# Query projections as seven block products, late groups behind the residual, and two MLPs in program order

## The chip, the cores and the metric

The kernel runs on one core of a Trainium2 chip. The metric is the device time of one execution in microseconds (us). The same kernel was timed three times; the median is the figure that counts.

## The reference

The program is a two-layer decoder trunk over 1024 tokens of width 1024, in float32. Each layer is a mixer, a cross-attention into 256 memory tokens and a squared-ReLU MLP, each behind an RMS norm and with a residual add. Layer 0 mixes by differential attention and pooling, layer 1 by a gated short convolution.

```python
def cross_attention(h, mem_n, wq, wkv, wo):
    q = (h @ wq).reshape(B, S, X_HEADS, X_HEAD_DIM)          # 1024 x 1024 @ 1024 x 1024, 4 heads of 256
    kv = (mem_n @ wkv).reshape(B, M, 2, X_HEADS, X_HEAD_DIM)
    s = jnp.einsum('bshd,bmhd->bhsm', q, kv[:, :, 0]) * X_HEAD_DIM ** -0.5
    p = jax.nn.softmax(s, axis=-1)
    o = jnp.einsum('bhsm,bmhd->bshd', p, kv[:, :, 1]).reshape(B, S, D_MODEL)
    return o @ wo

def sq_relu_mlp(h, w1, w2):                                  # 1024 -> 4096 -> 1024
    a = jax.nn.relu(h @ w1)
    return (a * a) @ w2

# layer l:  h += mixer(rms_norm(h)); h += cross_attention(rms_norm(h), ...); h += sq_relu_mlp(rms_norm(h), ...)
```

## The kernel before

**Operands.** The hidden state is kept transposed: 8 tiles of 128 features by 1024 tokens. Every operand of a large product is cut into a high part (rounded, by ACT) and a low part (the rest, by DVE, `cut`), and a product takes three matmuls: high by high, high by low, low by high. Weights are loaded in an order written out once (`order`); `w_load` keeps up to four raw tiles in flight on the SP queue, and `w_cut` cuts one weight tile ahead of its use into two rotating buffers (`wh`, `wl`). `w_next` hands out the next cut tile and cuts one more.

**Plain products.** `gemm` computes one 128-feature output tile: 8 input tiles x 3 parts x 2 halves of 512 tokens, so 48 matmuls of 128x512 (L189). The query projections of both cross-attentions, the output projections and the convolution's projections are of this kind.

**Block products.** Both MLP products go by `split_gemm` (L265): two output tiles and two token halves make a 2x2 block, got from seven products of sums of blocks instead of eight. One call has 7 steps of 4 x 3 = 12 matmuls. The sums of weight blocks are formed on POOL inside `w_cut` (L149 to L153, four operations of 128x512 for a pair of weight tiles), the sums of activation blocks on DVE in `combine`; `Split` holds the four groups of cut activations. After step i, `out(i)` adds the step's PSUM bank into its result (`evac`), as listed in `ADDS`; the banks are few, so step i+2 often has to wait until step i's bank was read. Hooks, small functions keyed by step, are run ahead of a step's matmuls and place other work there: the norm's transposes (`stage1`, `stage2`), squares and stores of the MLP's first product, loads and cuts of its second product's operand.

**The residual** (`residual`) runs an output projection, adds the loaded hidden state, and prepares the next operand: with `split=True` the four groups of a `Split`, pair by pair of tiles, otherwise plain cut tiles. The two residuals ahead of the MLPs are split; the two ahead of the cross-attentions (named `X1` and `cvo`) are not. In the last tile of a split residual the halves are done one after the other, then all four groups, the last squares of the norm and the store follow.

**Cross-attention** (`cross`): `query(n)` for n = 0 to 6, `score(0)`, `query(7)`, and then eight units (4 heads x 2 token halves) of score, softmax, transpose and product with V. `kv_get(c)` loads the keys and values of two heads and cuts them, the low part on POOL (L873): once after query 3, once after `score(1)`.

**Order.** The order of instructions on each engine comes from a scheduler that plays the program through with modelled durations and picks by priority (the program's order) what is ready. Only the first stage is under `tc.manual_schedule(engines=IN_ORDER)`, where PE, DVE and ACT take the program's order. All activations live in 44 slots of 128x1024.

## Time and profile before

| | us |
|---|---|
| median of three runs | 2615.15 (2613.42 to 2619.64) |
| profiled execution | 2622.43 |
| its span, first to last instruction | 2620.6 |
| PE busy | 2541.0 (97%) |
| DVE / ACT / POOL busy | 1641.9 (63%) / 1009.8 (39%) / 694.4 (26%) |

The profile is one execution. PE is the matmul engine, DVE the vector, ACT the scalar, POOL the GpSimd engine, SP issues DMAs. A row of the timeline has its start, its duration, the engine, the line of the kernel and `output<-inputs`; a bracket at its end tells how long the engine was idle before it, and who ended that. The clock column of a stage is the share of the full matmul clock that was granted. Names carry the stage: `c0q` are the queries of cross-attention 0, `c0s` its scores, `c0po` its product with V, `c0o` its residual, `m0a` and `m0b` the first and second product of MLP 0; `c1` and `m1` are those of layer 1.

### The profile page before, as it was taken

The page shows a single profiled execution, that of the slowest core. Times are in us where ns is not written, and L with a number is a line of the kernel's source. Part 1 is how long each engine was busy: PE and PEld are TensorE (multiplying, and loading weights), DVE is VectorE, ACT ScalarE, POOL GpSimd, SP SyncE. Part 2 cuts the span into 40 slices and gives each one's busy share as a digit, 9 for nine tenths or more (in the row PEclk, how much of TensorE's full clock was granted, in tenths as well). Part 3 has the DMA queues.
Part 4 walks back from the last instruction along what each step waited for, and adds up shares of the span by engine and source line. Part 5 has one row for each costly group of instructions (what it writes and reads, how often), then busy time and mean ns, then how long its engine had stood idle before and what let it go on. Part 6 is the DMA issues. An engine that isn't in the chain of part 4 may idle for free.

```text
span 2620.6 us, 29978 instructions
## 1 busy us (share of the span) xinstructions
PE 2541.0 (97%) x11618; PEld 2076.6 (79%) x11618; DVE 1641.9 (63%) x1846; ACT 1009.8 (39%) x1389; POOL 694.4 (26%) x417
## 2 busy tenths in 40 slices
PE   7999999999999999999999999999999999999997
PEld 5777778888878888777788888888887888777786
DVE  7777764325567778877773333323566777877875
ACT  4554564225443334433342111222443433433432
POOL 3222100200233334323352111111032333422334
PEclk9999999999999999999999999999999999999998
DMA  5101146311324445777742111422133344777752
GB/s 170 33 25 49 52 160 211 112 66 51 114 89 144 149 161 212 282 266 248 256 143 73 49 49 51 145 82 70 49 121 113 141 158 159 261 268 241 264 203 95
DMA packets 108430, 365.89 MB, mean 140 GB/s; under 512 B 12416, under 2 KB 14848, under 8 KB 108288
## 3 DMA queue, kind: packets, MB, share of 16 engines
q1 hardware_dynamic: 74880, 252.82, 28.7%
q10 hardware_dynamic: 33408, 111.16, 11.1%
q8 instruction: 91, 1.49, 0.2%
q14 instruction: 51, 0.42, 0.1%
HBM read 249.91 MB, written 114.03 MB: 139 GB/s over the span
## 4 chain that ended last, share of the span: by engine, by line
PE 81%; DVE 7%; issue 6%; DMA 3%; ACT 2%; SPq 0%; POOL 0%; DVEq 0%; ACTq 0%; POOLq 0%
PE m1a_x L265 7%; PE m0a_x L265 7%; PE m1a_yz L265 5%; PE m0a_yz L265 5%; PE m1b_x L265 5%; PE m0b_x L265 4%; PE m1b_yz L265 4%; PE cvo L189 3%; PE X L189 3%; PE c0o L189 3%; PE c1o L189 3%; PE m0b_yz L265 3%; PE c1q L189 3%; PE c0q L189 3%; PE qkv L189 3%
## 5 line engine op out<-in xcount | busy, mean ns | idle before, releaser
L72 ACT ACTIVATE wh<-wr 128x1024 fp32r<-128x1024 f32 (+1 forms) x310 | 301.0, 971 | 953.5 <-PE m0b_yz L265 154.9
L73 DVE TENSOR_TENSOR wl<-wr,wh 128x1024 fp32r<-128x1024 f32 (+1 forms) x310 | 361.5, 1166 | 210.6 <-ACT wh L72 209.8
L152 POOL TENSOR_TENSOR wr<-wr,wr 128x512 f32<-128x512 f32 x63 | 88.7, 1408 | 703.0 <-DVE wl L73 703.0
L73 DVE TENSOR_TENSOR wl<-wt,wh 128x1024 fp32r<-128x1024 f32 x64 | 135.7, 2120 | 4.8 <-ACT wh L72 4.6
L153 POOL TENSOR_TENSOR wr<-wr,wt 128x512 f32<-128x512 f32 x63 | 125.8, 1997 | 0.0
L150 POOL TENSOR_TENSOR wt<-wr,wt 128x512 f32<-128x512 f32 x63 | 119.9, 1904 | 4.8
L149 POOL TENSOR_TENSOR wt<-wr 128x512 f32<-128x512 f32 x63 | 90.5, 1436 | 92.0 <-issue 65.3
L72 ACT ACTIVATE wh<-wt 128x1024 fp32r<-128x1024 f32 x64 | 67.4, 1054 | 55.6 <-PE m0b_x L265 20.4
L1117 POOL TENSOR_TENSOR cv_z<-cv_z,cv_cg 128x1024 f32<-128x1024 f32 x8 | 26.2, 3276 | 175.4 <-DVE cv_z L1116 175.4
L565 ACT ACTIVATE s_p<-s,s_negm 128x128 f32<-128x128 f32 (+7 forms) x64 | 47.2, 740 | 29.1 <-DVE s_negm L564 26.1
L976 DVE SCALAR_TENSOR_TENSOR m1a_r<-m1a_r,c1o_rbc 128x1024 f32<-128x1024 f32 x32 | 52.2, 1636 | 0.9
L976 DVE SCALAR_TENSOR_TENSOR m0a_r<-m0a_r,c0o_rbc 128x1024 f32<-128x1024 f32 x32 | 52.2, 1636 | 0.9
L977 ACT ACTIVATE m1a_r<-m1a_r 128x1024 f32<-128x1024 f32 x32 | 33.9, 1061 | 42.6 <-DVE m1a_r L976 42.6
L977 ACT ACTIVATE m0a_r<-m0a_r 128x1024 f32<-128x1024 f32 x32 | 33.9, 1061 | 42.4 <-DVE m0a_r L976 42.4
L308 POOL TENSOR_TENSOR X_acc<-X_acc,X_sq 128x1024 f32<-128x1024 f32 x7 | 17.5, 2497 | 123.2 <-ACT X_sq L307 123.2
L564 DVE TENSOR_REDUCE s_negm<-s 128x1 f32<-128x128 f32 (+7 forms) x64 | 46.5, 749 | 0.2
L843 DVE TENSOR_TENSOR X1h<-X1h,X 128x1024 f32<-128x1024 f32 x8 | 9.8, 1221 | 58.0 <-PE X L189 58.0
L843 DVE TENSOR_TENSOR cvoh<-cvoh,cvo 128x1024 f32<-128x1024 f32 x8 | 9.8, 1221 | 57.3 <-PE cvo L189 57.3
L991 DVE TENSOR_TENSOR m1a_r<-m1a_r,m1a_yz 128x512 f32<-128x512 f32 x32 | 22.0, 686 | 36.6 <-PE m1a_yz L265 36.6
L991 DVE TENSOR_TENSOR m0a_r<-m0a_r,m0a_yz 128x512 f32<-128x512 f32 x32 | 22.0, 687 | 36.6 <-PE m0a_yz L265 36.6
L577 DVE SCALAR_TENSOR_TENSOR s_p<-s_p,rden,s_p 128x128 f32<-128x128 f32 (+7 forms) x32 | 36.0, 1125 | 6.4 <-ACT s_p L576 6.2
L308 POOL TENSOR_TENSOR c1o_acc<-c1o_acc,c1o_sq 128x1024 f32<-128x1024 f32 x6 | 15.5, 2588 | 91.0 <-ACT c1o_sq L307 91.0
(2717 smaller groups left out, 7986.9 us busy)
## 6 DMA issues: line engine op xcount, KB each, us to landing
wr<-in_w_dram SPq DMA_DIRECT2D x128, 512.0 KB, 3.8
m0f<-m0a_d SPq DMA_DIRECT2D x48, 512.0 KB, 5.9
m1f<-m1a_d SPq DMA_DIRECT2D x48, 512.0 KB, 6.1
wr<-in_wkv_dram SPq DMA_DIRECT2D x32, 512.0 KB, 3.5
m0a_d<-m0a_r ACTq DMA_DIRECT2D x32, 512.0 KB, 2.9
m1a_d<-m1a_r ACTq DMA_DIRECT2D x32, 512.0 KB, 2.9
wr<-in_conv_in_dram SPq DMA_DIRECT2D x24, 512.0 KB, 3.5
wr<-in_wq_dram SPq DMA_DIRECT2D x16, 512.0 KB, 3.6
```

The lines of the kernel that those rows point to most:

```text
L72: nc.scalar.activation(hi, src, AF.Copy)
L73: nc.vector.tensor_sub(lo, src, f32(hi))
L149: nc.gpsimd.tensor_add(t[:, 4:], b[:, :4], b[:, 4:])
L150: nc.gpsimd.tensor_sub(t[:, :4], a[:, :4], t[:, 4:])
L152: nc.gpsimd.tensor_sub(a[:, :4], b[:, :4], a[:, :4])
L153: nc.gpsimd.tensor_add(a[:, 4:], a[:, 4:], t[:, :4])
L189: nc.tensor.matmul(ps, wt[:, k, :], act.part(k, i, h), start=(k == 0 and wt is hi and i == 0), stop=(k == ks - 1 and wt is lo))
L265: nc.tensor.matmul(banks[b], w[a][:, 4 * (i % 2) + j, :], act.part(g, s, j, c), start=(new and j == 0 and n == 0), stop=(j == nk - 1 and n ...
L564: nc.vector.tensor_reduce(s["negm"][:, m : m + 1], ps[:, :L], axis=AX.X, op=ALU.max, negate=True)
L565: nc.scalar.activation(s["pr"][m][:, :L], ps[:, :L], AF.Exp, bias=s["negm"][:, m : m + 1], accum_out=s["den"][:, m : m + 1])
L976: nc.vector.scalar_tensor_tensor(v, v, 0.0, b(), op0=ALU.max, op1=ALU.mult)
L977: nc.scalar.activation(t, t, AF.Square)
```

## The change

1. `wq` is loaded in pairs of tiles with their features in the order that block products need, and `query(p)` makes two output tiles by one `split_gemm`: four calls of 84 matmuls in place of eight products of 48, in each of the two layers. The residuals `X1` and `cvo` are split. Their input `Y` becomes `Halves`: a slot holds the high and low part of one token half, so that slots come free half by half.
2. In the last tile of a split residual, groups 2 and 3, the norm's last squares and the store are left for hooks of steps 2, 3 and 4 of the next block product (`X.late`); one more weight cut is put there (`w_cut`). The MLP's `stage1` moves from step 4 to step 5.
3. `kv_get` runs at steps 2 and 4 of the last query pair, its low parts on DVE; `score(0)` stands ahead of that pair's last step.
4. `out` runs under `tc.high_priority()`.
5. Both MLPs are under `manual_schedule`: PE, DVE and ACT in the program's order.

```diff
-        order += [(FLAT, wq[l, n]) for n in range(KT)]
+        order += [(FLAT, wq[l, 2 * p], wq[l, 2 * p + 1]) for p in range(KT // 2)]
...
+    class Halves(Act):
+        def put(self, name, k, src):
+            t = [slot(f"{name}{k}_{h}", F32R) for h in range(2)]
+            self.t[k] = t
+            for h in range(2):
+                cut(t[h][:, :H], t[h][:, H:], src[:, half(h)])
+        def part(self, k, i, h):
+            return self.t[k][h][:, i * H : (i + 1) * H]
...
         def out(i):
-            for n, h in (TAIL_ADDS if tail else ADDS)[i]:
-                evac(n, h, banks[(TAIL if tail else SPLIT)[i][2]], (n, h) not in seen)
-                seen.add((n, h))
+            with tc.high_priority():
+                for n, h in (TAIL_ADDS if tail else ADDS)[i]:
+                    evac(n, h, banks[(TAIL if tail else SPLIT)[i][2]], (n, h) not in seen)
+                    seen.add((n, h))
...
                     if h == 0:
                         nx.group(0, j, r[0])
                         nn.add(t[:, half(h)], h, last=True)
+                    else:
+                        w_cut()
...
-                for g, raw in ((1, tt), (2, r[1]), (3, t4[:, :H])):
-                    nx.group(g, j, raw)
+                nx.group(1, j, tt)
+                if n < KT - 1:
+                    nx.group(2, j, r[1])
+                    nx.group(3, j, t4[:, :H])
             if split and n == KT - 1:
-                nn.add(t[:, half(1)], 1, last=True)
-            h_store(n, t, name)
+                nx.late = {2: [lambda: nx.group(2, j, r[1])], 3: [lambda: nn.add(t[:, half(1)], 1, last=True)],
+                           4: [lambda: nx.group(3, j, t4[:, :H]), lambda: h_store(n, t, name)]}
+            else:
+                h_store(n, t, name)
...
-                nc.gpsimd.tensor_sub(kvp[cc][1], t, f32(kvp[cc][0]))
+                nc.vector.tensor_sub(kvp[cc][1], t, f32(kvp[cc][0]))
...
-        def query(n):
-            ps = gemm(X, f"{name}q{n}", {5: nrm.stage1} if n == 0 else None)
-            Q.t[n] = pair(f"{name}q{n}")
-            cut(*Q.t[n], ps)
+        def query(p, hooks):
+            r = [slot(f"{name}q{p}_r{n}") for n in range(2)]
+            for n in range(2):
+                Q.t[2 * p + n] = pair(f"{name}q{2 * p + n}")
+            def evac(n, h, ps, new):
+                q, d = [x[:, half(h)] for x in Q.t[2 * p + n]], r[n][:, half(h)]
+                if (n, h) == (1, 0):
+                    cut(*q, ps)
+                elif new:
+                    nc.scalar.activation(d, ps, AF.Copy)
+                else:
+                    nc.vector.tensor_add(d, d, ps)
+                    if (n, h) == (1, 1):
+                        cut(*q, d)
+                    elif h == 1:
+                        cut(*Q.t[2 * p], r[0])
+            split_gemm(X, f"{name}q{p}", evac, hooks, first=(p == 0))
...
-        score(0)
-        query(KT - 1)
+        for p, hooks in enumerate((merged(X.late, {5: [nrm.stage1]}), {1: [divide]}, {},
+                                   {2: [lambda: kv_get(0)], 4: [lambda: kv_get(1)], 6: [lambda: score(0)]})):
+            query(p, hooks)
         norm_p(0)
         for u in range(n + 1):
             if u + 1 < n:
                 score(u + 1)
-                if u == 0:
-                    kv_get(1)
...
-        rest, ahead = {4: [nrm.stage1], 6: [nrm.stage2]}, []
+        rest, ahead = merged(X.late, {5: [nrm.stage1], 6: [nrm.stage2]}), []
...
-        Y = Act()
+        Y = Halves()
...
-        return residual(Y, g_next, f"{name}o")
+            Y.put(f"{nm}g", j, y)
+        return residual(Y, g_next, f"{name}o", split=True)
...
-    X, nrm = mlp(0, X, nrm, G_MIX[1], "m0")
+    with tc.manual_schedule(engines=IN_ORDER):
+        X, nrm = mlp(0, X, nrm, G_MIX[1], "m0")
```

The second MLP is put under `manual_schedule` in the same way.

More of the change, by code (lines that the diff above doesn't have):

```diff
@@ L289, in split_gemm, with merged @@
                 out(i)
+    def merged(*hooks):
+        return {i: [f for h in hooks for f in h.get(i, ())] for i in range(7)}
     class Norm:
@@ L795, in hybrid_trunk @@
             k = (0, 1, 2, 4, 5, 6, 7, 3)[i // YGAP]
-            Y.t[k] = pair(f"Y{k}")
-            cut(*Y.t[k], o_t[k] if k < 4 else y_t[k - 4])
+            Y.put("Y", k, o_t[k] if k < 4 else y_t[k - 4])
     hd = {n: xT[n] for n in range(KT)}
@@ L854, in residual @@
                 combine(r[0], r[1], tt, t4[:, :H])
-                for g, raw in ((1, tt), (2, r[1]), (3, t4[:, :H])):
-                    nx.group(g, j, raw)
+                nx.group(1, j, tt)
+                if n < KT - 1:
+                    nx.group(2, j, r[1])
+                    nx.group(3, j, t4[:, :H])
             if split and n == KT - 1:
-                nn.add(t[:, half(1)], 1, last=True)
-            h_store(n, t, name)
+                nx.late = {2: [lambda: nx.group(2, j, r[1])], 3: [lambda: nn.add(t[:, half(1)], 1, last=True)],
+                           4: [lambda: nx.group(3, j, t4[:, :H]), lambda: h_store(n, t, name)]}
+            else:
+                h_store(n, t, name)
         return nx, nn
-    X, nrm = residual(Y, G_X[0], "X1")
+    X, nrm = residual(Y, G_X[0], "X1", split=True)
     def cross(l, X, nrm, g_next, name):
@@ L872, in kv_get, with divide @@
                 nc.scalar.activation(kvp[cc][0], t, AF.Copy)
-                nc.gpsimd.tensor_sub(kvp[cc][1], t, f32(kvp[cc][0]))
+                nc.vector.tensor_sub(kvp[cc][1], t, f32(kvp[cc][0]))
         rc = small.tile([P, KT], F32, tag="rc16", name=f"{name}_rc16")
         Q = Act()
-        def query(n):
-            ps = gemm(X, f"{name}q{n}", {5: nrm.stage1} if n == 0 else None)
-            Q.t[n] = pair(f"{name}q{n}")
-            cut(*Q.t[n], ps)
-            if n == 1:
-                nc.vector.tensor_scalar_mul(rc, nrm.rcol, 1.0 / 16.0)
-            if n == 3:
-                kv_get(0)
-        for n in range(KT - 1):
-            query(n)
+        def query(p, hooks):
[15 more added lines that the diff above has]
+            split_gemm(X, f"{name}q{p}", evac, hooks, first=(p == 0))
+        def divide():
+            nc.vector.tensor_scalar_mul(rc, nrm.rcol, 1.0 / 16.0)
         units = [(h, th) for h in range(4) for th in range(2)]
@@ L1024, in ready @@
             return run
-        def merged(*hooks):
-            return {i: [f for h in hooks for f in h.get(i, ())] for i in range(7)}
         def prepare(c, left):
@@ L1105, in conv_mixer @@
         hooks = with_norm(nrm)
-        Y = Act()
+        Y = Halves()
         for j in range(KT):
@@ L1126, in conv_mixer @@
             nc.vector.tensor_mul(y, y, psb_)
-            Y.t[j] = pair(f"{nm}g")
-            cut(*Y.t[j], y)
-        return residual(Y, g_next, f"{name}o")
+            Y.put(f"{nm}g", j, y)
+        return residual(Y, g_next, f"{name}o", split=True)
     X, nrm = cross(0, X, nrm, G_MLP[0], "c0")
-    X, nrm = mlp(0, X, nrm, G_MIX[1], "m0")
+    with tc.manual_schedule(engines=IN_ORDER):
+        X, nrm = mlp(0, X, nrm, G_MIX[1], "m0")
     X, nrm = conv_mixer(X, nrm, G_X[1], "cv")
     X, nrm = cross(1, X, nrm, G_MLP[1], "c1")
-    _, fn = mlp(1, X, nrm, None, "m1")
+    with tc.manual_schedule(engines=IN_ORDER):
+        _, fn = mlp(1, X, nrm, None, "m1")
     SHARED = (4, 5)
@@ L1202, in _layout @@
     g["conv_out"] = tiles(a["conv_w_out"][0])
-    g["wq"] = tiles(a["xattn_wq"])
     g["wkv"] = a["xattn_wkv"].reshape(2, 4, 2, P, 4, H).transpose(0, 4, 1, 3, 2, 5)
@@ L1207, in _layout @@
     halves = [0, 2, 4, 6, 1, 3, 5, 7]
+    g["wq"] = tiles(a["xattn_wq"])[..., halves, :]
     g["w1"] = tiles(a["mlp_w1"])[..., halves, :]
     g["w2"] = tiles(a["mlp_w2"].reshape(2, 4, D, D))[..., halves, :]
-    return {n: np.ascontiguousarray(v) for n, v in g.items()}
+    names = ("xT memT vecs lams rel onehot negrow invcnt w_qk0 w_in w_out pool_w conv_in conv_out "
+             "wq wkv wo w1 w2").split()
+    return {n: np.ascontiguousarray(g[n]) for n in names}
 def kernel(**inputs):
```

## The prediction, made before the changed kernel was run

> **What bounds the kernel now.** I read the busy line, then the chain that ended last, then the stages, and last the timeline at each place where a stage is longer than its matmuls.
>
> ```profile
> PE 2541.0 (97%) x11618; PEld 2076.6 (79%) x11618; DVE 1641.9 (63%) x1846; ACT 1009.8 (39%) x1389; POOL 694.4 (26%) x417
> PE 81%; DVE 7%; issue 6%; DMA 3%; ACT 2%; SPq 0%; POOL 0%; DVEq 0%; ACTq 0%; POOLq 0%
> ```
>
> PE has 97% of the span and 81% of the chain: a matmul that goes away is worth its own time, unless its neighbours stop fitting under PE. The table by stage (length, then busy us per engine, the clock third from the end) tells where PE loses time today:
>
> ```profile
> core 0: us, PE busy (x) PEld busy (x) DVE busy (x) ACT busy (x) POOL busy (x), PEclk, DMA share, GB/s
> 421.14:508.18 87.04, 87.04 (x385) 72.12 (x385) 26.72 (x22) 24.17 (x25) 14.93 (x6) 1.00 0.43 150
> 508.18:585.07 76.89, 76.89 (x345) 63.76 (x344) 19.43 (x19) 16.91 (x18) 8.98 (x4) 1.00 0.21 69
> 585.07:653.41 68.34, 62.84 (x379) 55.44 (x378) 41.83 (x77) 34.16 (x89) 4.75 (x2) 0.95 0.16 55
> 746.07:772.36 26.29, 23.13 (x97) 18.73 (x96) 16.91 (x19) 9.99 (x15) 6.04 (x4) 0.87 0.18 60
> 772.36:1059.04 286.68, 286.68 (x1262) 235.45 (x1261) 222.04 (x214) 116.20 (x141) 104.64 (x60) 1.00 0.48 170
> 1059.04:1380.22 321.18, 309.60 (x1346) 251.20 (x1345) 245.02 (x249) 127.09 (x139) 116.68 (x67) 1.00 0.67 237
> ```
>
> The residual `X1` (421 to 508) and the queries (508 to 585) have no idle PE and a DVE used for a quarter to a third. Attention (585 to 653) loses 5.5 us and some clock. The seam into the MLP (746 to 772) loses 3.2 us and runs at 0.87 of the clock. The MLP's first product loses nothing, with DVE at 222 of 287 us. The second (1059 to 1380) leaves PE idle for 11.6 us. Layer 1 repeats these stages nearly to the tenth.
>
> **The change part by part.** The profiled execution took 2622.4 us (span 2620.6), 7.3 above the median of 2615.15; I sum against the former and carry the difference over.
>
> *Fewer matmuls.* One plain output tile, one step of a block product, one plain query stage; then DVE's cut of a tile and its add of a half out of PSUM, as groups:
>
> ```profile
> 1414.68 10.88 PE cv1c L189 x48
> 775.24 2.72 PE m0a_yz L265 x12
> 515.86 68.94 PE c0q L189 x304
> L73 DVE TENSOR_TENSOR wl<-wr,wh 128x1024 fp32r<-128x1024 f32 x9 | 11.0, 1225 | 59.8 <-ACT wh L72 59.8
> L991 DVE TENSOR_TENSOR m1a_r<-m1a_r,m1a_yz 128x512 f32<-128x512 f32 x32 | 22.0, 686 | 36.6 <-PE m1a_yz L265 36.6
> ```
>
> The first three give 0.2267 us a matmul. Eight query tiles are 384 matmuls, four block products are 336: 48 x 0.2267 = 10.9 us a layer, 21.8 in all. What comes with it: per pair three and a half weight cuts and two query tiles' cuts of 1.2 us and three adds of 0.7, 8.7 us of DVE, and four POOL sums, in 19 us of PE. The MLP's first product carries more per pair (222/15 = 14.8 of 19.1) with no idle PE, so I cost it at nothing; uncovered it would be 8 x 8.7 us.
>
> *Keys and values.* This is where attention loses its time, shown by DVE's, POOL's and PE's timelines and the chain:
>
> ```profile
> 588.19 1.22 DVE L908 TENSOR_REDUCE c0s_mx<-c0s 128x4 f32<-128x1024 f32 x1
> 592.23 1.14 DVE L922 TENSOR_SCALAR c0s_p<-c0s_p,c0rd 128x256 f32<-128x256 f32 x4
> 607.60 5.33 DVE L922 TENSOR_SCALAR c0s_p<-c0s_p,c0rd 128x256 f32<-128x256 f32 x4
> 607.51 2.40 POOL L873 TENSOR_TENSOR c0kv1l<-c0kv,c0kv1h 128x1024 fp32r<-128x1024 f32 x1 [44.42 <-ACT c0kv1h L872]
> 609.86 2.40 POOL L873 TENSOR_TENSOR c0kv3l<-c0kv,c0kv3h 128x1024 fp32r<-128x1024 f32 x1
> 614.99 0.80 PE L943 MATMUL c0po<-c0pt0l,c0kv2h 128*128 128x512 f32 x1 [4.58 <-DVE c0pt0l L73]
> 614.99 5.06 PE c0po L943 x11
> 631.67 2.88 PE c0s L904 x24
> ```
>
> The same four scalings take 1.14 us alone and 5.33 while POOL cuts keys: DVE is held until both POOL operations (2 x 2.40) are over, the cut of the first probabilities queues behind it, and PE waits 4.6 us. Then 11 matmuls take 5.06 us in place of 2.5, the clock being down after the wait. Together 7.1 us, and layer 1 shows the same. [...]
>
> With the low parts on DVE this goes. The four loads move up past SP's loads of the output weights, into the last query pair. `score(0)` needs the first keys at that pair's step 6, 4 x 2.72 = 10.9 us after the hook; a load takes 4.5 us to land, two cuts about 2.3:
>
> ```profile
> c0kv<-kv_d SPq DMA_DIRECT2D x4, 512.0 KB, 4.5
> ```
>
> The four DVE cuts (4.9 us) lie in the last pair, whose DVE load becomes some 15 of 19 us. What is late next is the first softmax. From its reduce to the end of the scalings it takes 593.37 - 588.19 = 5.2 us; before, query 7 (10.9 us) and the next score covered that, now only step 6 and the next score (2.72 + 2.88 = 5.6). It just fits, unless the last query's cuts stand in front of the reduce. Bounds: 0, and the 7.1 of today as the nearest wait at that place; I take 1 us, nearer to the cover that fits. So -12.2 for both layers.
>
> *Seams into the queries.* `X1` and `cvo` become split residuals, with 4 sums and 1.5 more cuts a pair in stages where DVE is used 27 of 87 us: hidden (uncovered some 4 x 4.6 us each). `Halves` turns a cut of 1.2 into two of 0.7 for eight tiles, in stages with the same idle DVE; priority and load order add no instruction and no byte. At their end the queries start as the MLP starts today. Today's plain seam costs 0, the MLP's seam this much (ACT's queue, then PE):
>
> ```profile
> 750.79 1.06 ACT L72 ACTIVATE c0o_x_3h<-c0o_r 128x1024 fp32r<-128x1024 f32 x1 [0.73 <-DVE c0o_r L249]
> 751.75 1.04 ACT L72 ACTIVATE wh<-wr 128x1024 fp32r<-128x1024 f32 x1
> 752.70 0.61 ACT L72 ACTIVATE c0o_x<-c0o_t 128x512 fp32r<-128x512 f32 x1
> 753.22 0.61 ACT L307 ACTIVATE c0o_sq<-c0oh 128x512 f32<-128x512 f32 x1
> 753.74 0.57 ACT L987 ACTIVATE m0a_r<-m0a_x 128x512 f32<-128x512 f32 x1
> 754.36 0.80 PE L265 MATMUL m0a_x<-c0o_x_0h,wh 128*128 128x512 f32 x1 [3.16 <-ACT m0a_r L987]
> ```
>
> PE waits 3.16 us for one copy out of PSUM that stands behind groups 2 and 3, a weight cut and a square, and the stage's clock of 0.87 costs 0.13 x 23.1 = 3.0 more: 6.2. These groups, the square and the store are just what is now left for later, and the copy has priority. Bounds 0 and 6.2; 1.5 each, nearer to nothing, since the copy's blockers are named and moved: +3.0.
>
> *Seams into the MLPs.* The same 6.2 goes, twice. But `stage1` now stands one step ahead of `stage2` in place of two, and PE, held to the program, must wait for the norm between them:
>
> ```profile
> 764.07 0.68 DVE L317 TENSOR_REDUCE c0o_ms<-c0o_n 128x4 f32<-128x512 f32 x1
> 765.04 1.65 POOL L320 TENSOR_TENSOR c0o_rcol<-c0o_ms,mhalf 128x8 f32<-128x8 f32 x1 [13.24 <-DVE c0o_ms L319]
> ```
>
> Two reduces and the power are 0.7 + 0.7 + 1.65 = 3.0 us against a step of 2.72, and a DVE add of 0.7 comes first: 1 us of wait (0, or 3 if two POOL sums stand ahead). Net -5.2 twice: -10.4.
>
> *First product in the program's order.* One pair of the steady state, on DVE, POOL and ACT:
>
> ```profile
> 904.21 1.23 DVE L976 SCALAR_TENSOR_TENSOR m0a_r<-m0a_r,c0o_rbc 128x1024 f32<-128x1024 f32 x1
> 907.20 1.88 DVE L976 SCALAR_TENSOR_TENSOR m0a_r<-m0a_r,c0o_rbc 128x1024 f32<-128x1024 f32 x1
> 909.01 2.32 DVE L73 TENSOR_TENSOR wl<-wt,wh 128x1024 fp32r<-128x1024 f32 x1
> 911.46 1.29 POOL L149 TENSOR_TENSOR wt<-wr 128x512 f32<-128x512 f32 x1 [1.22 <-issue]
> 912.83 2.17 POOL L150 TENSOR_TENSOR wt<-wr,wt 128x512 f32<-128x512 f32 x1
> 909.12 1.06 ACT L977 ACTIVATE m0a_r<-m0a_r 128x1024 f32<-128x1024 f32 x1 [1.64 <-DVE m0a_r L976]
> 911.53 1.06 ACT L72 ACTIVATE wh<-wr 128x1024 fp32r<-128x1024 f32 x1 [0.87 <-PE m0a_yz L265]
> ```
>
> Today the rescalings (L976) run before the third weight tile is cut; the program puts the second one behind it. From the start of step 2, in order: weight high 1.06, weight low 1.22, rescaling 1.23, ACT's square 1.06, and only then ACT's copy 0.57, which step 4 needs 2 x 2.72 = 5.44 later. The chain is 5.14: it fits by 0.3. But beside POOL a DVE operation is longer by 1.10 (2.32 for 1.22) or 0.65 (1.88 for 1.23). In program order the cut of `wt` goes on as today, from 1.1 us into the pair to 3.4; L149 comes after it, waits for a rescaling (to 4.6), and L150 ends near 7.1. The weight's low part could start at 5.44 + 1.06 + 0.1 = 6.6 and is held for 0.5: 0.2 too late. Bounds: 0, and two holds of 1.1 less 0.3, 1.9. I take 0.2, by the order just worked out: 15 pairs x 2 MLPs x 0.2 = +6.0. Behind that copy on ACT stand only the next weight's high part and the stores' DMAs, which have a step to spare.
>
> *Second product in the program's order.* PE's waits today are for the adds out of PSUM:
>
> ```profile
> PE m0b_yz L265 <- DVE m0b1h L1064: 1.9, 2, 1.4
> m0f<-m0a_d SPq DMA_DIRECT2D x48, 512.0 KB, 5.9
> ```
>
> They fall where a new quarter of the operand begins. There, in program order, DVE has in five steps (13.6 us): five cuts of 1.22, four of half that, three weight cuts and five adds, 6.1 + 2.4 + 3.7 + 3.4 = 15.6, and up to three holds of 1.1 by POOL: 18.9. Less the 13.6 and the 2 by which an add may be late (2.72 less its 0.7), that is 0 to 3.3 us. Four quarters: 0 to 13, and today's 11.6 lies inside. Loads (5.9 us) are issued three steps (8.2 us) ahead, so a cut held to its place waits for none, unless SP's queue is 2 us late. I take no change: 0, with -11.6 and, since the quarter before may leave DVE behind, +6 as ends per MLP.
>
> Sum: -21.8 - 12.2 + 3.0 - 10.4 + 6.0 + 0 = -35.4; 2622.4 - 35.4 = 2587.0 for an execution like the profiled one, 2615.2 - 35.4 = 2579.8 against the median.
>
> **The rivals.** *Order helps the second product.* Its adds no longer stand behind the scheduler's misjudged cuts: both MLPs lose 11.6 less, 2579.8 - 23.2 = 2556.6. For it: every wait there is for a DVE add, at boundaries that repeat alike. Against: DVE's load at a boundary exceeds PE's.
>
> *The seams do not close.* Scheduling outside the MLPs still follows modelled durations, which do not know POOL's hold. The queries start as the MLPs did (6.2 twice in place of 3.0: +9.4), and attention waits for its first probabilities as long as before (7.1 in place of 1, twice: +12.2): 2601.4. For it: today's scheduler made both waits; against: the blockers are moved. A PE wait of 3.16 us was enough to bring the stage's clock to 0.87. [...]
>
> *Slower: POOL holds the program's order.* If two POOL sums fall into the chain of every first-product pair, each pair loses 1.9 us: 30 x 1.9 = 57 in place of 6, 2630.8. From 1.6 us a pair on the change is slower by over 0.3%. For it: 2.32 and 1.88 show two holds in each pair today; against: the chain begins only at step 2, when L149 is mostly over.
>
> *The order does not bind*, and the MLPs run as today, seams included: 2579.8 + 10.4 - 6.0 = 2584.2; same range.
>
> **How the numbers follow.** Forecast 0.52 (2570 to 2592), order helps 0.20, seams stay open 0.12, the order does not bind 0.08, POOL holds 0.08. The range takes in the second and third with some spread and leaves out the slower rival: 2553 to 2606. A measurement of this kernel can tell 0.3%, 7.8 us: faster means under 2607.3, slower above 2623.0. Faster: all of the first, second and fourth, and half of the third, 0.86. The rest of the third and a weak form of the hold are no change, 0.08; slower 0.06.
>
> **What would show it.** Queries of 76 us a layer with PE busy throughout; no POOL row beside the scalings, each near 1.14 us, no 4.6 us wait for `c0pt0l`; the copy out of step 0 at both kinds of seam within 0.3 us of its matmuls, clock near 1.00 there; the first product's pairs at 19.2 us, with waits for ACT's copy at step 4. I am wrong if these waits exceed 1 us, if DVE waits for `m0f` loads in its order, or if the second product's idle time leaves 0 to 18 us.

## The result, and the profile after

| | median of the runs, us | ratio to before | 95% interval |
|---|---|---|---|
| before | 2615.82 (2613.42 to 2619.64) | | |
| after | 2598.22 (2597.53 to 2598.74) | 0.9931 | 0.9914 to 0.9948 |

The change gains 17.6 us, where 35.4 were forecast. The two profiled executions, 2622.4 and 2598.7 us, differ by 23.7; the kernel before spreads over 10 us from run to run (its medians in the four later comparisons are 2620.4, 2619.6, 2617.2 and 2619.8), and its granted clock goes with that: there the executions under 2618 us had a clock of 0.992 to 0.994, those above it 0.989 to 0.992. The working below goes by stages of the profiled executions, since these can be laid side by side.

The busy line of the page after, and the windows of the kernel after, each from the first matmul of a stage to the first of the next (columns as in the prediction's table: start:end, length, busy us, the clock third from the end): residual `X1`, queries, attention, first and second product of MLP 0, convolution mixer.

```profile
PE 2515.8 (97%) x11522; PEld 2055.6 (79%) x11522; DVE 1687.0 (65%) x1972; ACT 1067.7 (41%) x1503; POOL 688.7 (27%) x439
420.21:501.81 81.60, 81.60 (x362) 67.57 (x360) 46.15 (x39) 35.48 (x43) 18.18 (x8) 1.00 0.44 155
501.81:583.85 82.04, 80.50 (x358) 65.90 (x356) 50.07 (x53) 34.80 (x47) 26.98 (x16) 1.00 0.24 77
583.85:635.39 51.54, 48.65 (x313) 44.31 (x312) 35.91 (x73) 31.59 (x83) 0.00 (x0) 0.93 0.18 63
727.35:1047.19 319.84, 316.17 (x1386) 258.07 (x1384) 221.84 (x238) 130.78 (x159) 98.61 (x67) 0.99 0.46 159
1047.19:1367.75 320.56, 308.24 (x1346) 251.24 (x1344) 240.43 (x247) 123.08 (x137) 110.40 (x67) 1.00 0.64 234
1367.75:1632.77 265.02, 263.16 (x1169) 217.79 (x1168) 91.07 (x83) 47.04 (x52) 53.32 (x19) 1.00 0.19 60
```

PE lost 96 matmuls (11618 to 11522) and 25 us of busy time. The same lengths for every kernel, in us, are the thread through the rest, a block of numbers per layer. "Start" is the length of the first stage, in which the change alters hardly more than how `Y` is cut. "Queries" is residual plus queries, `cv` the convolution mixer, `m1a` and `m1b` the products of MLP 1; the tail runs from the last norm's first transposes to the end. The residuals between attention and MLP are left out: they take 91.9 to 92.2 us in every kernel. The attention column begins with the first scores, so it holds 48 matmuls of the last query in the kernel before, 36 in 2 and 9, and 12 in the others; compare queries and attention by their sum.

| kernel | start | queries | attention | m0a | m0b | cv | queries 1 | attention 1 | m1a | m1b | tail |
|---|---|---|---|---|---|---|---|---|---|---|---|
| before | 421.0 | 164.1 | 62.5 | 319.5 | 321.0 | 262.9 | 164.1 | 62.5 | 319.8 | 318.5 | 20.7 |
| after | 420.2 | 163.6 | 51.5 | 319.8 | 320.6 | 265.0 | 163.7 | 50.8 | 319.6 | 316.4 | 21.7 |
| 1 late sums | 420.6 | 162.1 | 49.4 | 315.6 | 320.5 | 265.0 | 162.0 | 51.4 | 315.6 | 316.4 | 21.3 |
| 2 early score | 419.6 | 158.3 | 55.3 | 319.8 | 320.5 | 265.0 | 158.3 | 55.5 | 318.3 | 316.5 | 21.7 |
| 3 no order | 419.9 | 163.7 | 50.5 | 315.7 | 321.0 | 262.9 | 163.7 | 51.5 | 315.8 | 317.7 | 20.7 |
| 4 keys on POOL | 419.7 | 163.7 | 48.1 | 320.7 | 320.5 | 265.0 | 163.7 | 48.1 | 319.5 | 316.4 | 21.4 |
| 5 no priority | 420.6 | 163.7 | 50.5 | 318.1 | 320.5 | 266.6 | 163.7 | 50.5 | 320.8 | 316.4 | 21.7 |
| 6 no POOL sums | 420.7 | 161.8 | 50.8 | 314.4 | 307.8 | 266.6 | 161.8 | 51.6 | 314.4 | 305.0 | 20.9 |
| 7 = 1 + 4 | 422.2 | 162.0 | 48.1 | 315.6 | 320.6 | 266.6 | 162.0 | 48.1 | 315.6 | 316.4 | 20.9 |
| 8 = 7 + 3 | 418.2 | 162.0 | 48.1 | 314.3 | 321.0 | 263.0 | 162.0 | 48.1 | 314.3 | 317.1 | 20.7 |
| 9 = 8 + 2 | 423.1 | 156.6 | 54.5 | 314.3 | 320.5 | 263.0 | 156.5 | 57.1 | 314.3 | 317.4 | 20.7 |
| 10 = 8, sums on DVE | 419.6 | 162.0 | 48.1 | 315.7 | 316.5 | 263.0 | 162.0 | 48.1 | 315.8 | 307.9 | 20.7 |
| 11 = 10 with order | 419.9 | 162.0 | 48.1 | 319.3 | 325.1 | 265.0 | 162.0 | 48.1 | 319.2 | 322.8 | 21.3 |
| 12 = 10, second product only | 418.8 | 162.0 | 48.1 | 314.6 | 317.7 | 263.0 | 162.0 | 48.1 | 314.6 | 308.1 | 20.7 |

Queries and attention together gained 11.4 us in layer 0 and 12.2 in layer 1; the two first products, which hold the MLP seams, gained nothing (+0.3 and -0.2).

**The seam into the MLP, after.** First the chain of waits' two entries, PE's and the norm's, then DVE, POOL, ACT and PE in order of time:

```profile
PE m0a_yz L277 <- DVE m0a_r L1025: 3.4, 1, 3.4
PE c0o_b L345 <- POOL c0o_rcol L336: 0.3, 1, 0.3
...
736.69 1.78 DVE L261 TENSOR_TENSOR c0o_r<-c0o_r 128x512 f32<-128x512 f32 x1
738.39 1.75 DVE L262 TENSOR_TENSOR c0o_t<-c0o_r,c0o_t 128x512 f32<-128x512 f32 x1
740.07 1.21 DVE L73 TENSOR_TENSOR c0o_x_3l<-c0o_t,c0o_x_3h 128x1024 fp32r<-128x1024 f32 x1
741.20 0.67 DVE L1025 TENSOR_TENSOR m0a_r<-m0a_r,m0a_yz 128x512 f32<-128x512 f32 x1
...
736.59 1.33 POOL L149 TENSOR_TENSOR wt<-wr 128x512 f32<-128x512 f32 x1 [5.54 <-issue]
738.00 1.60 POOL L150 TENSOR_TENSOR wt<-wr,wt 128x512 f32<-128x512 f32 x1
...
737.99 0.60 ACT L1021 ACTIVATE m0a_r<-m0a_x 128x512 f32<-128x512 f32 x1
...
741.93 0.79 PE L277 MATMUL m0a_yz<-c0o_x_0h,wh 128*128 128x512 f32 x1 [3.36 <-DVE m0a_r L1025]
742.52 0.63 PE L277 MATMUL m0a_yz<-c0o_x_0l,wh 128*128 128x512 f32 x1
```

ACT's copy, which the kernel before waited for, now runs at 737.99, while PE is still at the next bank. PE waits 3.36 us (3.16 before) for the evacuation behind it: DVE's add at 741.20. It stands behind the last two sums of `combine` and a cut of group 1, and the sums take 1.8 us each beside POOL's weight sums. The matmuls that follow come every 0.43 us in place of 0.23 until 745.07.

**Attention, after:** PE's wait, then DVE and ACT around the first softmax.

```profile
PE c0s L939 <- ACT c0s_p L948: 2.3, 2, 2.2
...
586.06 1.22 DVE L895 TENSOR_TENSOR c0kv1l<-c0kv,c0kv1h 128x1024 fp32r<-128x1024 f32 x1
587.19 1.22 DVE L943 TENSOR_REDUCE c0s_mx<-c0s 128x4 f32<-128x1024 f32 x1
588.44 0.16 DVE L944 TENSOR_TENSOR c0s_mx<-c0s_mx,c_rc 128x4 f32<-128x4 f32 x1
...
595.42 1.14 DVE L957 TENSOR_SCALAR c0s_p<-c0s_p,c0rd 128x256 f32<-128x256 f32 x4
...
589.44 1.06 ACT L72 ACTIVATE wh<-wr 128x1024 fp32r<-128x1024 f32 x1 [2.28 <-PE c0q_x L277]
...
592.36 0.55 ACT L948 ACTIVATE c0s_p<-c0s,c0s_mx,c_rc 128x256 f32<-128x256 f32 x1
```

The scalings take their 1.14 us and no 4.6 us wait is left, as forecast. But the maximum is ready at 588.6 and the first exponential starts at 592.36: ACT holds a weight cut that waits 2.28 us for PE's last query step, and behind it three cuts of the last query tiles.

**Two more waits after**, at the start of the queries and behind MLP 0:

```profile
PE c0q_yz L277 <- DVE c0q_r L912: 1.5, 1, 1.5
...
PE m0b_n L332 <- POOL m0b_acc L324: 1.9, 1, 1.9
```

### The profile page after: what moved, and what is told of

Same layout as the page of the kernel before. It is cut to its first block, busy times and chain, and to the rows that moved or that the text cites. A ratio compares the mean times of both kernels' runs of the same rounds, so it can differ in the third digit from the quotient of the medians.

```text
span 2597.0 us, 30119 instructions
## 1 busy us (share of the span) xinstructions
PE 2515.8 (97%) x11522; PEld 2055.6 (79%) x11522; DVE 1687.0 (65%) x1972; ACT 1067.7 (41%) x1503; POOL 688.7 (27%) x439
## 5 line engine op out<-in xcount | busy, mean ns | idle before, releaser
L73 DVE TENSOR_TENSOR wl<-wr,wh 128x1024 fp32r<-128x1024 f32 (+1 forms) x318 | 373.2, 1174 | 98.9 <-ACT wh L72 98.5
L152 POOL TENSOR_TENSOR wr<-wr,wr 128x512 f32<-128x512 f32 x71 | 106.0, 1493 | 792.3 <-DVE wl L73 788.3
L149 POOL TENSOR_TENSOR wt<-wr 128x512 f32<-128x512 f32 x71 | 126.3, 1779 | 135.7 <-issue 88.1
L73 DVE TENSOR_TENSOR wl<-wt,wh 128x1024 fp32r<-128x1024 f32 x72 | 146.5, 2035 | 17.0 <-ACT wh L72 17.0
L150 POOL TENSOR_TENSOR wt<-wr,wt 128x512 f32<-128x512 f32 x71 | 105.9, 1492 | 5.3
L153 POOL TENSOR_TENSOR wr<-wr,wt 128x512 f32<-128x512 f32 x71 | 105.5, 1485 | 0.0
L201 PE MATMUL X<-Y,wh 128*128 128x512 f32 x256 | 69.8, 389 | 0.0
L201 PEld LDWEIGHTS X<-Y,wh 128*128 128x128 f32 x256 | 48.0, 188 | 10.2 <-DVE X1h L851 0.3
L324 POOL TENSOR_TENSOR c0o_acc<-c0o_acc,c0o_sq 128x1024 f32<-128x1024 f32 x6 | 15.5, 2591 | 119.5 <-ACT c0o_sq L323 119.5
L201 PE MATMUL X<-Y,wl 128*128 128x512 f32 x128 | 40.7, 389 | 0.0
```

The source lines that it names most:

```text
L73: nc.vector.tensor_sub(lo, src, f32(hi))
L149: nc.gpsimd.tensor_add(t[:, 4:], b[:, :4], b[:, 4:])
L150: nc.gpsimd.tensor_sub(t[:, :4], a[:, :4], t[:, 4:])
L152: nc.gpsimd.tensor_sub(a[:, :4], b[:, :4], a[:, :4])
L153: nc.gpsimd.tensor_add(a[:, 4:], a[:, 4:], t[:, :4])
L201: nc.tensor.matmul(ps, wt[:, k, :], act.part(k, i, h), start=(k == 0 and wt is hi and i == 0), stop=(k == ks - 1 and wt is lo))
```

## The experiments

Medians are compared with the kernel after (2598.22, ratio 0.9931); each ratio is to the kernel before, timed beside it. That kernel's median was 1.4 to 4.6 us higher in these comparisons than beside the kernel after, so by the ratios each kernel comes out better by as much; differences of a few us are read by stage.

**1. Two of the four sums and group 1 later.**

```diff
-                combine(r[0], r[1], tt, t4[:, :H])
-                nx.group(1, j, tt)
+                combine1(r[0], r[1], tt)
                 if n < KT - 1:
+                    combine2(r[0], r[1], tt, t4[:, :H])
+                    nx.group(1, j, tt)
                     nx.group(2, j, r[1])
...
-                nx.late = {2: [lambda: nx.group(2, j, r[1])], 3: ...
+                nx.late = {2: [lambda: nx.group(1, j, tt), lambda: combine2(r[0], r[1], tt, t4[:, :H]),
+                               lambda: nx.group(2, j, r[1])], 3: ...
```

> Edit: at the end of a split residual only the first two of the four sums of its last pair of tiles (those of group 1) stay in front; the other two sums, and the cuts of groups 1 and 2, go behind step 2 of the next product. Theory (the wait at the seam is the queue of VectorE in front of its add, two sums of 1.8 us that POOL's sums stretch and a cut of 1.2 us): the add comes about 4.5 us earlier, PE's 3.36 us wait in front of the first steps of each MLP falls under 1 us, and the steps at the low clock after it go too: 4 to 5 us at each of the two MLP seams, up to 1 us at each query seam, 8 to 12 us in all (ratio to the changed kernel 0.9953 to 0.997; about 2586 to 2590 us). Rival A (the wait moves on: step 2 or 3 then needs group 1 or 2, cut later): PE waits as long one step further on, within 3 us of the changed kernel. Rival B (the seam is held by POOL's sums themselves, not by what stands in VectorE's queue): the wait stays on the same add and nothing moves.

2585.9 us, ratio 0.9872 (0.9858 to 0.9885): 12.3 less than after. DVE and PE at the same seam, and the first product's window:

```profile
732.79 0.68 DVE L259 TENSOR_TENSOR c0o_t<-c0o_t,c0o_r 128x512 f32<-128x512 f32 x1
735.38 0.69 DVE L1032 TENSOR_TENSOR m0a_r<-m0a_r,m0a_yz 128x512 f32<-128x512 f32 x1 [1.91 <-PE m0a_yz L282]
...
736.12 0.50 PE L282 MATMUL m0a_yz<-c0o_x_0h,wh 128*128 128x512 f32 x1 [0.85 <-DVE m0a_r L1032]
...
724.05:1039.65 315.60, 314.44 (x1385) 257.01 (x1384) 219.95 (x238) 130.70 (x159) 98.24 (x67) 1.00 0.47 161
```

DVE now waits for PE in front of the add, PE waits 0.85 us in place of 3.36, and the matmuls behind that wait come every 0.23 us (clock of the window 1.00, 0.99 in the kernel after). The first products lose 4.2 and 4.0 us, both query stages 1.6. The theory holds in place and size (8 to 12 us were expected; these stages give 11.4), and both rivals fall. The attentions moved by -2.1 and +0.6, with their clocks: 0.93 and 0.97 in the kernel after, 1.00 and 0.93 here (-2.3 and +0.9 us of PE busy time).

**2. The first scores two steps earlier.**

```diff
-  {2: [lambda: kv_get(0)], 4: [lambda: kv_get(1)], 6: [lambda: score(0)]}
+  {2: [lambda: kv_get(0)], 4: [lambda: score(0), lambda: kv_get(1)]}
```

> Edit: the first scores are computed behind step 4 of the last pair of query tiles, ahead of the load of the second keys and values, instead of behind step 6. Theory (PE's 2.3 us wait at the start of the attention, and the 0.84 us behind it, is the first softmax, whose exponentials stand in ACT's queue behind the cuts of the last query tiles): with the scores two steps earlier and the exponentials ahead of those cuts, PE still has query steps to run; about 3 us less in each layer, 5 to 6.5 us in all (about 2592 to 2593 us). Rival A (the scalings now stand in front of VectorE's last adds of the query, which come 4 to 5 us later and hold a bank or the cut that a later score needs): the wait comes back in front of the scores, no change within 2 us. Rival B (the second unit's softmax is what is late): only the 2.3 us moves on, no change.

2598.33 us, ratio 0.9916 (0.9903 to 0.993): no change that the intervals can tell; by stage, queries and attention are 1.6 and 0.7 us shorter, which is within the scatter of the attention (2.2 us, see 4). PE's wait in the attention, and DVE's first scalings and two maxima:

```profile
PE c0s L939 <- ACT c0s_p L948: 2.7, 1, 2.7
...
580.93 1.23 DVE L943 TENSOR_REDUCE c0s_mx<-c0s 128x4 f32<-128x1024 f32 x1 [0.26 <-PE c0s L939]
...
584.98 1.14 DVE L957 TENSOR_SCALAR c0s_p<-c0s_p,c0rd 128x256 f32<-128x256 f32 x4
...
593.51 1.22 DVE L943 TENSOR_REDUCE c0s_mx<-c0s 128x4 f32<-128x1024 f32 x1
```

The first softmax is over at 586, long before PE needs it. Now PE waits 2.7 us for the second unit's exponentials, whose maximum stands on DVE behind the cuts of keys, weights and query tiles. Rival B.

**3. No program order in the MLPs.**

```diff
-    with tc.manual_schedule(engines=IN_ORDER):
-        X, nrm = mlp(0, X, nrm, G_MIX[1], "m0")
+    X, nrm = mlp(0, X, nrm, G_MIX[1], "m0")
```

(and likewise for MLP 1)

> Edit: the two blocks that hold the MLPs' instructions on PE, VectorE and ACT in the program's order are taken out, all else as changed. Forecast on record: the first product pays about 6 us for the order (0.2 us a pair), the second nothing, so without the order about 6 us faster (2592 us). By the changed trace's own periods (19.16 us a pair against 19.04) it would be 3.6 us at most. Rival A (the order helps the second product's quarter boundaries, where 2 us a layer came): 3 to 10 us slower. Rival B (the planner's order is the same, but for a few instructions): within 2 us. Rival C (the seams into the MLPs need the order): the 6.2 us seams get longer, and that alone makes it slower.

2588.62 us, ratio 0.9881 (0.9867 to 0.9894): 9.6 less. Waits at the MLP seam, the mixer's window, and POOL's first norm sum there, without and then with the order:

```profile
PE m0a_yz L277 <- DVE m0a_r L1025: 1.6, 1, 1.6
...
1362.80:1625.74 262.94, 262.94 (x1170) 217.87 (x1168) 90.61 (x83) 46.45 (x52) 52.02 (x19) 1.00 0.18 59
...
1363.30 2.54 POOL L324 TENSOR_TENSOR m0b_acc<-m0b_acc,m0b_sq 128x1024 f32<-128x1024 f32 x1 [8.66 <-ACT m0b_sq L323]
```

```profile
1369.92 6.59 POOL L324 TENSOR_TENSOR m0b_acc<-m0b_acc,m0b_sq 128x1024 f32<-128x1024 f32 x2 [9.37 <-ACT m0b_sq L323]
```

The first products gain 4.1 and 3.9. Counted by the steps from matmul to matmul beyond 0.2267 us, 3.3 of the 4.1 is the seam: the scheduler lets PE go on with more of the other steps, so it waits 1.6 us there for the same add. The pairs give 0.8, not 3. The mixer gives back 2.1 and the tail 1.0. In the mixer PE's norm waits for POOL's sum, which starts 2.2 us after the mixer's first matmul with the order and 0.5 without. The second products pay 0.5 and 1.3. So the order cost the change about 9 us; the forecast's 6 was sought in the pairs, and none of the theories named more than a part of the rest.

**4. Keys' and values' low parts on POOL, at the new place.**

```diff
-                nc.vector.tensor_sub(kvp[cc][1], t, f32(kvp[cc][0]))
+                nc.gpsimd.tensor_sub(kvp[cc][1], t, f32(kvp[cc][0]))
```

> Edit: the low parts of keys and values go back to POOL, but stay where the change put them (behind steps 2 and 4 of the last query pair). Theory (the engine matters: POOL's subtraction beside the scalings stretched them, and PE waited for them): 2 to 3 us slower in each layer, 4 to 6 us in all (about 2603 us). Rival (the place was all of it: two steps earlier POOL is done before the first scalings, and VectorE has two cuts less in front of the first maximum): within 2 us, or 1 to 3 us faster.

2593.18 us, ratio 0.9897 (0.9884 to 0.9911): 5.0 less. PE's wait, DVE, POOL and ACT around the first maximum, and the attention's window:

```profile
PE c0s L939 <- ACT c0s_p L948: 1.7, 1, 1.7
...
586.52 1.23 DVE L943 TENSOR_REDUCE c0s_mx<-c0s 128x4 f32<-128x1024 f32 x1 [0.78 <-PE c0s L939]
587.78 0.96 DVE L944 TENSOR_TENSOR c0s_mx<-c0s_mx,c_rc 128x4 f32<-128x4 f32 x1
...
586.33 2.40 POOL L895 TENSOR_TENSOR c0kv3l<-c0kv,c0kv3h 128x1024 fp32r<-128x1024 f32 x1 [2.97 <-ACT c0kv3h L894]
...
589.76 0.56 ACT L948 ACTIVATE c0s_p<-c0s,c0s_mx,c_rc 128x256 f32<-128x256 f32 x1
...
583.45:631.57 48.12, 45.89 (x314) 41.52 (x312) 34.45 (x69) 29.89 (x81) 2.40 (x1) 1.00 0.18 62
```

The rival holds, with more than it asked for: the attentions are 3.4 and 2.7 us shorter. POOL is done at 588.7, before any scaling, and costs DVE 0.8 us there: the small product of 0.16 us takes 0.96 and ends with POOL. So moving the loads did all the good. How the cuts on DVE did harm is only in part shown. Two of them, of 1.2 us, stood ahead of the first two maxima, yet the first maximum was ready at 588.6, and here at 588.7. What differs is ACT: its first exponential starts at 589.76 in place of 592.36, with one cut between PE's last query step and it in place of four, since the scheduler ordered ACT anew too. Of the 3.4 us in layer 0, 2.8 are busy time of the same matmuls (48.65 to 45.89), at a clock of 0.93 after and 1.00 here. With these cuts on DVE the attention took 49.4 to 51.6 us in five kernels (the one after, 1, 3, 5 and 6), at clocks of 0.93 and 0.97 in the one after, 1.00 and 0.93 in 1, 0.97 in 5; on POOL it takes 48.1 each time (clock 1.00 in 4, 7 and 8), unless the scores come early (9).

**5. No priority for the evacuations.**

```diff
-            with tc.high_priority():
-                for n, h in (TAIL_ADDS if tail else ADDS)[i]:
+            for n, h in (TAIL_ADDS if tail else ADDS)[i]:
```

> Edit: the seven block products' evacuations without the high priority, all else as changed. Theory (the priority only matters where the planner chooses, that is at the end of a stage into the queries; inside the MLPs the program's order holds): up to 1.5 us more at each query seam and 1 us in the attention, nothing in the MLPs: 1 to 5 us slower than the changed kernel (2597 span). Rival A (the planner had put the copies in time without it, since the groups behind them are now later in the program): within 1 us. Rival B (the priority pulls adds ahead of cuts that PE needs sooner): 1 to 4 us faster.

2597.86 us, ratio 0.9918 (0.9905 to 0.9932): no change, rival A. The query stages are the same to 0.1 us. Attention, `m0a`, `m1a` and the mixer moved by up to 1.7 us either way, with the same waits in `m0a` and the mixer; these are the stages that wait 1.86 to 3.4 us in the kernel after, see the last section.

**6. POOL's weight sums left out.**

```diff
                 raw.append(t)
-                nc.gpsimd.tensor_add(t[:, 4:], b[:, :4], b[:, 4:])
-                nc.gpsimd.tensor_sub(t[:, :4], a[:, :4], t[:, 4:])
                 cut(hi, lo, a)
-                nc.gpsimd.tensor_sub(a[:, :4], b[:, :4], a[:, :4])
-                nc.gpsimd.tensor_add(a[:, 4:], a[:, 4:], t[:, :4])
```

(In place of the scratch tile `t`, the raw tile `b` is appended. The kernel leaves the sums out, so its products of the third and fourth weight groups are of other numbers; it only prices the sums.)

> Edit: POOL's four sums on each weight tile of the seven products are left out (the third and fourth weight groups then hold the raw tile, so the products of those groups are of other numbers); ACT's and VectorE's work is as it was. It measures what POOL costs the other engines. Theory (POOL's sums stretch VectorE's combining sums at a seam from about 1.2 to 1.8 us, and with them the wait in front of the MLP): VectorE's two sums of 1.8 us fall to about 1.2, PE's 3.4 us wait in front of each MLP to about 2, and 2 to 4 us go in all, with the MLPs' periods as they were. Rival A (POOL also holds the pairs and the four boundaries of the second product): 10 us or more. Rival B (POOL's sums stretch nothing that PE waits for): within 1 us, the seam as long as before.

2560.65 us, ratio 0.9776 (0.9763 to 0.979): 37.6 less. DVE and POOL of the kernel after, where a new quarter of the second product's operand begins; then the second product's window without the sums:

```profile
1129.36 2.32 DVE L73 TENSOR_TENSOR m0A_2l<-m0f,m0A_2h 128x1024 fp32r<-128x1024 f32 x1
1131.60 0.67 DVE L1095 TENSOR_TENSOR m0b0h<-m0b0h,m0b_x 128x512 f32<-128x512 f32 x1
1132.20 1.71 DVE L73 TENSOR_TENSOR wl<-wt,wh 128x1024 fp32r<-128x1024 f32 x1
...
1130.55 2.28 POOL L153 TENSOR_TENSOR wr<-wr,wt 128x512 f32<-128x512 f32 x1
```

```profile
1039.76:1347.53 307.77, 307.19 (x1345) 251.56 (x1344) 216.00 (x247) 123.10 (x137) 13.97 (x5) 1.00 0.67 243
```

Rival A: the seams gave what the theory said and more (first products -5.4 and -5.2), but the second products gave 12.8 and 11.4. At the seam the two sums take 0.69 us each without POOL (the expectation had 1.2), and PE waits 1.2 us in place of 3.36. In the second product, with the same instructions on DVE, its busy time falls from 240.4 to 216.0 us, and PE's idle time from 12.3 to 0.6. In the kernel after, PE waits there at each of the four quarters, about 1.5 us for a DVE add and 1.0 us for an ACT cut; both waits are gone. That fits the prediction's own sum for a quarter, 0 without POOL's holds and up to 3.3 us with them: 12.3 over four quarters is 3.1. The edit also takes away the time that others wait for the sums themselves; as far as the profile shows, these are two waits of ACT in this window, 2.4 us each, and none of PE.

**7 and 8. Late sums with the low parts on POOL (the diffs of 1 and 4), then without the order (that of 3 too).**

> Edit: both, the late sums at the end of a split residual and the low parts of keys and values on POOL. Theory (two separate queues, each in front of a different wait): the stages give what they gave apart, 1.6 us at each query stage, 3.4 and 2.7 in the attentions, 4.2 and 4.0 at the MLP seams: 18 us less than the changed kernel (about 2579 us, ratio to before about 0.985). Rival (they share VectorE's queue at the attention, where the late sums alone gave -2.1 and +0.6): the attentions give no more than the late sums did, 13 to 14 us less (about 2584 us).

2580.08 us, ratio 0.9854 (0.984 to 0.9867): 18.1 less than after. Queries, attentions and seams gave what they gave alone.

> Edit: the late sums, the low parts on POOL, and the MLPs without the program's order. Theory (of the 9.8 us that the order cost, 3.3 us at each MLP seam were the same wait that the late sums take away; left are 0.8 us a first product and 2.1 us behind the first MLP, against 0.5 and 1.3 us that the order gives in the second products): 2 to 3 us less than with the order (about 2576.5 us). Rival A (the two add up: the planner also shortens what the late sums leave): 8 us less than with the order. Rival B (with the seams mended the order is as good or better): the same, or up to 2 us more.

2577.45 us, ratio 0.9842 (0.9828 to 0.9855): 2.6 less, as forecast, though the intervals overlap. By stages of the profiled executions it is 1.3 in each first product, 3.7 in the mixer (1.6 of it busy time: 264.78 us at a clock of 0.99 in 7, for 263.16 at 1.00 in the kernel after), against 0.4 and 0.7 paid in the second products.

**9. And the early scores: the diffs of 1, 2, 3 and 4.**

> Edit: the version with late sums, low parts on POOL and no order in the MLPs, and with the first scores behind step 4 of the last query pair. Theory (with the low parts off VectorE the second unit's maximum, which took the wait over when the scores alone came early, stands behind two cuts less): about 1 to 2 us less in each attention, 2575 us. Rival (VectorE's three remaining cuts ahead of the second maximum still hold it, and the scalings ahead of the last query add delay that): the same within 1 us, or 1 us more.

2579.74 us, ratio 0.9853 (0.9838 to 0.9868): the rival. Queries and attention together are 1 and 3.5 us longer than in 8; PE waits 3.2 us for the second unit; ahead of its maximum two of DVE's cuts are longer beside POOL's cuts of the keys (2.35 us for 1.22, 2.01 for 0.69; POOL is busy for 6.43 us of that attention).

**10 to 12. The weight sums on DVE.**

```diff
             elif g == 0:
...
-                nc.gpsimd.tensor_add(t[:, 4:], b[:, :4], b[:, 4:])
+                nc.vector.tensor_add(t[:, 4:], b[:, :4], b[:, 4:])
```

(all four of them, on top of 8; in 11 with the order kept, that is on top of 7; 12 as follows)

```diff
+                eng = nc.vector if u in second else nc.gpsimd   # second: the units of w2
-                nc.gpsimd.tensor_add(t[:, 4:], b[:, :4], b[:, 4:])
+                eng.tensor_add(t[:, 4:], b[:, :4], b[:, 4:])
```

> Edit: the version with late sums, low parts on POOL and no order, with the four sums on each weight tile of the seven products on VectorE instead of POOL. Theory (VectorE and POOL wait for one another whenever both work from memory, so that a POOL sum of 1.1 us or more costs VectorE at least as long as doing it itself in about 0.65 us): VectorE's busy time in an MLP stays about the same (4 x 0.65 us a pair more, its stretched rows shorter by as much or more), and the second product's boundary waits of 1.6 and 1.2 us get smaller: 8 to 20 us less (2557 to 2569 us). Rival A (VectorE's queue now holds sums that wait for a weight's transfer, ahead of the adds that PE waits for): 10 us slower or more. Rival B (the boundaries are bound by VectorE's sum of work, wherever the sums run): within 4 us.

2566.2 us, ratio 0.9802 (0.9789 to 0.9815): 11.2 less than 8, inside the theory's 8 to 20. Second product of MLP 0 in 8 and in 10:

```profile
1034.88:1355.85 320.97, 308.84 (x1346) 251.16 (x1344) 245.75 (x249) 126.90 (x139) 117.92 (x67) 1.00 0.66 237
```

```profile
1037.65:1354.19 316.54, 309.12 (x1346) 252.59 (x1344) 255.94 (x311) 127.03 (x139) 13.60 (x5) 0.99 0.67 236
```

62 more instructions cost DVE 10 us, not the 43 that their 0.69 us each would make: the rest, 33 us, came back from its own rows, which less the 43 take 213 us, near the 216.0 of experiment 6 without the sums. POOL worked 104 us for the same sums. PE's idle time falls from 12.1 to 7.4 us here and from 11.1 to 3.7 in MLP 1.

> Edit: as the version with the weight sums on VectorE, but with the program's order in the MLPs. Theory (in the program's order a sum that waits for its weight's transfer cannot be put off, so it holds VectorE's queue at each unit): slower than the same without order by 3 us or more. Rival (weights are loaded a unit ahead, so nothing waits): within 3 us of it.

2599.12 us, ratio 0.9929 (0.9917 to 0.9941): 33 more than 10, in all four products and the mixer. PE's longest entry there is for a cut of the next operand:

```profile
PE m0b_x L282 <- ACT m0A_1h L72: 5.6, 3, 1.9
```

The direction was forecast, not the size. Which sum holds up which add in that order was not taken apart.

> Edit: the version with late sums, low parts on POOL, no order, and the weight sums on VectorE in the second products alone (in the queries and first products on POOL). Theory (the stages are separate: with all sums on VectorE the first products lost 1.45 and 1.54 us and the second products won 4.4 and 9.3): the first products go back to 314.3 us, the second products stay at 316.5 and 307.9: 3 us less than with all sums on VectorE, about 2563 us. Rival A (the second product's gain hangs on the first product's last sums too, which the planner places anew): 2 us more than that, 2566 us or above. Rival B (the planner's order changes in the first product as well): either way by up to 3 us.

2563.88 us, ratio 0.9789 (0.9775 to 0.9802). The first products are 1.2 us shorter, the second 1.2 and 0.2 longer: 1.8 of the 3 forecast in span, and not distinguishable from 10 by the intervals. These two are the fastest of the kernels that do the whole computation, 32 to 34 us below the changed kernel.

## Why the prediction was right or wrong

The direction and the range held; the size was half. That the range held is in part luck. The 2598.2 us lie outside the 2570 to 2592 of the forecast itself, and inside the range only because that took in the rival "the seams do not close", which had a chance of 0.12; and two terms that came out better than forecast, by 7.5 us together, cover part of the four that came out worse. Against the forecast's terms, in us by the profiled stages (a stage's loss is its length less 0.2267 us for each matmul that it has, so a stage with fewer matmuls can be compared):

| term | forecast | measured | settled by |
|---|---|---|---|
| 96 matmuls fewer | -21.8 | -21.8 (count and 0.2267) | the pages |
| keys and values | -12.2 | -2.8 and -3.6 | 2, 4 |
| seams into the queries | +3.0 | +2.3 twice | 1 |
| seams into the MLPs | -10.4 | -0.4 and -0.5 | 1, 3 |
| first product in order | +6.0 | +0.8 and +0.3 | 3 |
| second product in order | 0 | -0.5 and -2.1 | 3, 6 |
| mixer behind MLP 0, and tail | none | +2.1 and +1.0 | 3 |

The measured terms come to -22.9; the first stage's 0.8 is nearly all of the rest of the 23.7.

*Seams into the MLPs* is the step that failed, by 9.5 us. "The same 6.2 goes, twice" was read from the one evacuation that PE waited for. It did come promptly, 0.1 us behind the last matmul of its bank, as the prediction had asked for; the next one, on another engine, had a queue of its own that was as long. So two of the prediction's signs did not come: the clock in 26 us around the MLP seam was 0.94, not near 1.00 (0.87 before), and PE was not busy throughout the queries, with a wait of 1.5 us. The queue was to be seen in the code: the sums of the last pair stayed in front, and the prediction called such sums hidden by DVE's idle share of a stage (at `X1` and `cvo`, where DVE is used 27 of 87 us), while what counted was DVE's last 5 us of the stage. Experiment 1 moved two sums and a cut, and 8.2 us went.

*Keys and values* was mis-sized by 5.8 us. The mechanism, POOL holding the scalings, was right and is gone (5.33 us before, 1.14 after). The cover, "it just fits, unless the last query's cuts stand in front of the reduce", failed at another place: the maximum was ready at 588.6, but a weight cut and the last query's cuts stood on ACT ahead of the exponentials, until 592.36. On POOL, at the new place, the term is -6.2 twice: the forecast's size, by the opposite choice of engine. The tables of 2 and 9 show that earlier scores alone only pass the wait on.

*Seams into the queries* lay within its bounds, and 1.6 of the 2.3 is the same queue as at the MLPs.

*First product*: the chain that was worked out costs 0.02 to 0.05 us a pair, not 0.2. The norm's wait there is 0.3 us (`c0o_b` above), not 1. *Second product*: zero was about right, and so was its bound of 0 to 3.3 us a quarter, whose upper end is POOL's holds; experiment 6 shows that nearly all of the idle time goes with POOL's sums (12.3 to 0.6 us). The rival "order helps the second product" had put that idle time down to the scheduler; under the order it stayed. *The mixer* was not looked at: in the program's order the squares for the next norm come late, and POOL's sum with them.

Which of DVE's rows grow beside POOL can be read above: at 1131.60 the add out of PSUM takes its 0.67 us while POOL is at work, and the maximum at 586.52 its 1.23, where operations with two inputs in SBUF take 2.32 and 0.96 in place of 1.22 and 0.16. POOL's rows grow too, as in this part of the kernel after: 2.14 us, begun 0.2 us behind a cut of DVE that takes its 1.21, where a weight sum with no DVE row beside it takes 1.29 to 1.30.

```profile
1133.84 1.21 DVE L73 TENSOR_TENSOR m0A_3l<-m0f,m0A_3h 128x1024 fp32r<-128x1024 f32 x1
...
1134.05 2.14 POOL L149 TENSOR_TENSOR wt<-wr 128x512 f32<-128x512 f32 x1 [1.21 <-DMA m0f<-m0a_d]
```

In the kernel after, a weight sum and a DVE cut or combining sum overlap by more than 0.15 us in 193 places, and in 191 of them one of the two, or both, take over 0.08 us more than alone (1.30 for the sum, 1.23 or 0.70 for the row of DVE): the waiting for one another that the theory of 10 speaks of.

The rival "the seams do not close" (2601.4) came nearest in time and partly in place; "POOL holds the program's order" named the right engine, but the holds fall at the quarters of the second product and were there before the change.

## What to carry to other kernels

When a wait is removed, list every evacuation of the next two steps, engine by engine, with what is queued ahead of each; the gain is the wait less the next one, and a stage's mean idle share says nothing about its last microseconds. Before an operation is moved to another engine to free it from a collision, ask whether moving it in time is enough; here that alone was worth 1.3 to 3.5 us more a layer. A side engine beside which the loaded one's rows stretch (0.69 to 1.8 us here) is no free help: doing POOL's sums on the already busier DVE was 11.2 us faster, and a fixed program order has to be judged again after every such move.
